# A two-layer hybrid backbone: the order of the whole program from the scheduler's finer duration model

## The chip, the cores and the metric

One core of one Trainium2 chip runs the whole program in one launch. The metric is the device time of one execution in microseconds (us); the median of three runs of the kernel before is 3073.74 us (3067.39 to 3075.61).

## The reference

The reference computes two layers of a backbone for a diffusion generator on 1024 latent tokens and 256 context tokens of width 1024, all in float32. Cut to what matters:

```python
for i in range(2):                                   # layers; context is dropped after the first
    sh1, sc1, g1, sh2, sc2, g2 = split(silu(c) @ w_mod + b_mod)
    h = rms_norm(x, norm1_gain) * (1 + sc1) + sh1    # the same for the context tokens
    aq, ak, av, bq, bk, bv, cx, cg = split(h @ w_in)
    ya = diff_attention(...)    # 4 heads: softmax(q0 k0) - lam * softmax(q1 k1), all 1280 keys
    yb = window_attention(...)  # 6 heads: 256 context keys, 3 blocks of 128 keys, a sink
    yc = rglru(cx) * gelu(cg)   # a linear recurrence in both directions
    x = x + g1 * (concat(ya, yb, yc) @ w_out)
    h2 = rms_norm(x, norm2_gain) * (1 + sc2) + sh2
    gate, val = split(h2 @ w_up)                     # 2 x 2816 columns
    x = x + g2 * ((silu(dwconv(gate)) * val) @ w_down)
```

## The kernel before, in words

Every large matrix product is made in three passes: each factor is split in a rounded high part (`hi`, L184, on ACT) and the rest (`lo`, L187, on DVE or POOL), and high x high, high x low and low x high are added up in one PSUM bank. Each layer runs through these stages:

- **Phase A** (`phase_a`): norm, the input projection (`qkv`, L636 to L638), rope and per-head norms (`qk_post`), and the recurrence (`lru`). In the second layer the end of the first layer's down product (`tail`) comes ahead of it.
- **Phase B** (`phase_b`): windowed attention (`sw`), then differential attention (`da`). `da` is written as a software pipeline over query tiles, and it puts pieces of other work (modulation products, a part of the output projection) between its steps.
- **Phase C** (`phase_c`): output projection, second norm (`norm_ops`), then `up(f)` for 22 blocks of 128 gate and value columns, a Strassen-like scheme of seven products of sums of quarters (`t1` to `t4` are made on POOL, L1524, the activation sums on DVE, L1250 to L1264), and `down_steps`, the same scheme for the down product: five steps of seven products, each product's sums on POOL (L1342), splits on ACT, DVE and POOL, its result added from PSUM by DVE (L1380 into the residual, L1412 into a collected sum `a`). In the first layer the context tokens' products (`dc_ps`, L1425 to L1427) stand between them.

**What sets the order.** The kernel is written in a framework that has one in-order queue for each engine: PE (matmul), DVE, ACT, POOL, and SP, which issues most DMAs. The text of the kernel gives each instruction a place in the program. A scheduler then plays the program through before the launch: whenever a simulated engine is free, it takes the first instruction in program order whose inputs are ready and whose buffer is free at that simulated time. So an instruction can go ahead of one that stands before it in the program, if the simulation thinks that the earlier one has to wait. What comes out is a fixed order for each queue, with waits on semaphores. On the chip an engine never passes over an instruction that waits: what stands behind it waits too.

How long the simulation thinks that an instruction or a transfer takes decides the order. There are two such models. The coarse one is the default. The finer one follows an instruction through sequencer, queue, engine and semaphores. Before the change the finer one is asked for in one place, a block of its own around phase A of each layer and the tail ahead of it:

```python
    def layer(self, l):
        ...
        with self.tc.block(schedule_with_timeline_sim=True):
            if l:
                self.tail()
            self.phase_a()
        self.phase_b()
        self.phase_c()
```

A block is ordered by itself: nothing in it changes places with what stands outside. So the program falls into a short setup, block A of layer 0, phases B and C of layer 0 as one stretch, block A of layer 1 with the tail, and phases B and C of layer 1. Setup and the two B and C stretches were ordered with the coarse model.

The scheduler also gives out buffers in the order of its simulation. The tags that the prediction speaks of have few slots: PSUM has two banks of tag `t` and six of tag `p` in phase C.

## Time and profile before

| what | value |
|---|---|
| runs | 3067.39, 3073.74, 3075.61 us |
| the profiled execution | 3074.54 us, span 3072.8 us |
| mean granted TensorE clock | 0.972 of full speed |
| PE busy | 2836.2 us (92% of the span) |
| DVE, POOL, ACT busy | 2070.9 (67%), 1520.2 (49%), 1468.6 us (48%) |
| DMA | 349.25 MB, mean 114 GB/s |

The stages lie in the span about so: phase A of layer 0 from 0 to 337.5 us, windowed attention to 466, differential attention to 707, output projection and norm to 865, `up` to 1368, `down_steps` to 1661, tail and phase A of layer 1 to 1985, attention, output projection and norm of layer 1 to 2470, `up` to 2812, `down_steps` to 3046, and the last two of the 22 blocks to 3072.8.

A timeline row gives start, duration, engine, line, operation, the tile that is written and what is read; in square brackets stands how long the engine sat idle before it and what ended the wait. PE's busy time counts pipelined matmuls as one stretch. At full clock a 512-column matmul starts 0.23 us after the one before it.

### The profile page before, as it was taken

How to read it: one execution, taken by the hardware profiler on the slowest of the kernel's cores; microseconds unless marked ns; L12 is line 12 of the kernel's file. 1: busy time of each engine (PE TensorE's matmuls, PEld its weight loads, DVE VectorE, ACT ScalarE, POOL GpSimd, SP SyncE). 2: the span in 40 equal slices, each digit the busy share in tenths (PEclk: the TensorE clock that was granted, in tenths of full speed). 3: DMA queues.
4: the chain of work that ended last, by engine and by line, in shares of the span. 5: the costliest groups of instructions: out<-in, count | busy, mean ns of one | idle time of the engine just before them, and what ended most of it. 6: DMA issues, size and time to landing. Idle time of an engine off the chain costs nothing. (4 is left out here: it accounts for less than half of the span.)

```text
span 3072.8 us, 40965 instructions
## 1 busy us (share of the span) xinstructions
PE 2836.2 (92%) x15146; PEld 2308.8 (75%) x15146; DVE 2070.9 (67%) x2879; ACT 1468.6 (48%) x2450; POOL 1520.2 (49%) x1011
## 2 busy tenths in 40 slices
PE   6999898999899999998988899898999799999898
PEld 4798665678688888886877788666777678887776
DVE  6956656884854444457887985757885755556997
ACT  5544467784443433342332554567883444444331
POOL 4746412323554444448561765512323576665971
PEclk9999999999899999998999999999999999999999
DMA  7232627664122111143215331545533122224322
GB/s 254 83 85 82 173 61 248 185 196 172 38 81 76 67 68 67 67 182 113 83 56 192 112 109 52 145 109 168 130 121 131 55 89 83 83 83 158 123 83 83
DMA packets 208280, 349.25 MB, mean 114 GB/s; under 512 B 32720, under 2 KB 112336, under 8 KB 208080
## 3 DMA queue, kind: packets, MB, share of 16 engines
q1 hardware_dynamic: 203472, 331.69, 33.3%
q0 software_dynamic: 4608, 14.95, 2.2%
q8 instruction: 119, 1.95, 0.3%
q14 instruction: 81, 0.66, 0.1%
HBM read 257.19 MB, written 89.39 MB: 113 GB/s over the span
## 5 line engine op out<-in xcount | busy, mean ns | idle before, releaser
L184 ACT ACTIVATE w_r<-w_raw 128x512 fp32r<-128x512 f32 x338 | 212.7, 631 | 451.4 <-PE u_ps L1552 279.7
L1524 POOL TENSOR_TENSOR w_raw<-w_raw 128x512 f32<-128x512 f32 x176 | 249.9, 1425 | 229.3 <-DVE w_r L187 108.5
L187 DVE TENSOR_TENSOR w_r<-w_raw,w_r 128x512 fp32r<-128x512 f32 x206 | 151.3, 737 | 250.2 <-ACT w_r L184 250.1
L1551 PE MATMUL u_ps<-a,w_r 128*128 128x512 f32 x704 | 278.6, 396 | 5.1 <-DVE vb L1639 4.0
L1552 PE MATMUL u_ps<-a,w_r 128*128 128x512 f32 x704 | 277.5, 394 | 1.4 <-DVE a L187 1.2
L1553 PE MATMUL u_ps<-a,w_r 128*128 128x512 f32 x704 | 276.3, 392 | 0.0
L187 POOL TENSOR_TENSOR w_r<-w_raw,w_r 128x512 fp32r<-128x512 f32 x132 | 190.2, 1441 | 122.7 <-ACT w_r L184 117.5
L1403 PE MATMUL d_ps<-d_ah,d_b 128*128 128x512 f32 x560 | 225.2, 403 | 22.5 <-DVE xd L1380 12.3
L1404 PE MATMUL d_ps<-d_al,d_b 128*128 128x512 f32 x560 | 223.9, 400 | 6.2 <-DVE d_al L187 6.2
L946 DVE TENSOR_REDUCE da_sm<-da_s 128x1 f32<-128x1280 f32 (+1 forms) x144 | 194.9, 1367 | 43.6 <-PE da_s L936 42.7
L1405 PE MATMUL d_ps<-d_ah,d_b 128*128 128x512 f32 x560 | 223.3, 399 | 0.6 <-DVE d_b L187 0.6
L187 POOL TENSOR_TENSOR w<-raw,w 128x1024 fp32r<-128x1024 f32 (+2 forms) x62 | 141.1, 2283 | 144.1 <-ACT w L184 135.1
L953 ACT ACTIVATE da_e<-da_s,da_sm 128x1280 f32<-128x1280 f32 (+1 forms) x144 | 177.6, 1235 | 22.9 <-DVE da_sm L946 21.2
L1551 PEld LDWEIGHTS u_ps<-a,w_r 128*128 128x128 f32 x704 | 133.9, 190 | 34.6 <-DVE vb L1639 5.5
L1090 POOL TENSOR_TENSOR oy_x<-oy_x,oy_z 128x426 f32<-128x426 f32 (+3 forms) x48 | 52.1, 1086 | 216.3 <-ACT oy_z L1088 193.7
L1552 PEld LDWEIGHTS u_ps<-a,w_r 128*128 128x128 f32 x704 | 133.9, 190 | 29.5 <-DVE a L187 2.1
L1553 PEld LDWEIGHTS u_ps<-a,w_r 128*128 128x128 f32 x704 | 133.6, 190 | 28.8
L1380 DVE SCALAR_TENSOR_TENSOR xd<-d_ps,mods,xd 128x512 f32<-128x512 f32 x200 | 141.0, 739 | 19.7 <-PE d_ps L1405 19.4
L1403 PEld LDWEIGHTS d_ps<-d_ah,d_b 128*128 128x128 f32 x560 | 108.7, 194 | 48.3 <-DVE xd L1380 10.0
L936 PE MATMUL da_s<-dak,daq 96*128 96x512 f32 (+1 forms) x400 | 123.0, 395 | 13.7 <-ACT da_e L953 13.3
L1639 DVE TENSOR_TENSOR vb<-u_ps,vb 128x512 f32<-128x512 f32 x96 | 66.0, 688 | 99.2 <-PE u_ps L1553 90.5
L1551 PE MATMUL u_ps<-s_x,w_r 128*128 128x512 f32 x308 | 122.0, 396 | 10.1 <-ACT s_x L184 10.1
(349 smaller groups left out, 8616.3 us busy)
## 6 DMA issues: line engine op xcount, KB each, us to landing
wmod<-in_wmod SPq DMA_DIRECT2D x96, 512.0 KB, 6.5
w_raw<-in_wu SPq DMA_DIRECT2D x44, 1024.0 KB, 5.4
d_w<-in_wd SPq DMA_DIRECT2D x40, 512.0 KB, 3.9
d_a<-ud SPq DMA_DIRECT2D x40, 512.0 KB, 4.6
ud<-conv SPq DMA_DIRECT2D x22, 640.0 KB, 2.9
ud<-conv SPq DMA_DIRECT2D x22, 512.0 KB, 2.6
raw<-in_wg SPq DMA_DIRECT2D x16, 512.0 KB, 4.1
dak<-qk_da POOLq DMA_DIRECT2D x48, 160.0 KB, 4.6
```

Of the source, the lines that this page charges most:

```text
L184: self.nc.scalar.activation(out, in_, AF.Copy)
L187: (eng or self.nc.vector).tensor_tensor(out, in_, hi.bitcast(F32), ALU.subtract)
L946: nc.vector.tensor_reduce(st["sm"][:, mi:mi + 1], st["s"][mi][:, :b["nkc"]], AX.X, ALU.max, negate=True)
L953: nc.scalar.activation(e[:, :nkc], st["s"][mi][:, :nkc], AF.Exp, bias=st["sm"][:, mi:mi + 1], accum_out=b["s0"][:, ti, u["hd"], mi:mi + 1])
L1380: nc.vector.scalar_tensor_tensor(x, ps, gate, x, ALU.mult, ALU.add)
L1403: nc.tensor.matmul(ps, bh[:, w], ah[:, m], start=on is None and k == 0, stop=False, **kw)
L1404: nc.tensor.matmul(ps, bh[:, w], al[:, m], start=False, stop=False, **kw)
L1405: nc.tensor.matmul(ps, bl[:, w], ah[:, m], start=False, stop=k == 1, **kw)
L1524: sub = lambda o, a, b, op=ALU.subtract: nc.gpsimd.tensor_tensor(o, a, b, op)
L1551: nc.tensor.matmul(ps, wh[:, s], h, start=new and kk == 0, stop=False, skip_group_check=not new)
L1552: nc.tensor.matmul(ps, wh[:, s], lo, start=False, stop=False, skip_group_check=not new)
L1553: nc.tensor.matmul(ps, wl[:, s], h, start=False, stop=kk == 3, skip_group_check=not new)
```

## The change

One argument is given to the context that holds the whole program. Setup and both stretches of phases B and C are then ordered with the finer model too. No instruction is added or taken away, no tile changes its size; what changes is the order within each engine's queue, the buffers' turns, and with them the waits. The blocks stay, and nothing moves over their edges.

```diff
-    with tile.TileContext(nc) as tc:
+    with tile.TileContext(nc, schedule_with_timeline_sim=True) as tc:
         Build(tc, aps).run()
```

## Rows read from the trace of the kernel before

**Rows 1.** The page's first part: busy us, share of the span, instructions.

```profile
PE 2836.2 (92%) x15146; PEld 2308.8 (75%) x15146; DVE 2070.9 (67%) x2879; ACT 1468.6 (48%) x2450; POOL 1520.2 (49%) x1011
```

**Rows 2.** Windows by stage: length, busy PE, PEld, DVE, ACT, POOL; clock, DMA share, GB/s.

```profile
60.00:337.50 277.50, 262.37 (x1241) 224.21 (x1240) 200.85 (x264) 131.91 (x190) 176.90 (x98) 0.98 0.33 91
337.50:865.00 527.50, 476.27 (x3129) 363.15 (x3128) 360.40 (x618) 333.71 (x677) 161.75 (x158) 0.96 0.48 150
865.00:1368.00 503.00, 503.00 (x2672) 433.41 (x2671) 240.49 (x335) 203.67 (x326) 243.01 (x181) 1.00 0.23 82
1368.00:1661.00 293.00, 263.18 (x1329) 222.30 (x1327) 238.84 (x288) 84.88 (x99) 173.75 (x78) 0.96 0.30 99
1661.00:1985.00 324.00, 295.29 (x1416) 250.47 (x1414) 244.46 (x331) 158.70 (x233) 193.83 (x111) 0.95 0.41 121
1985.00:2470.00 485.00, 430.00 (x2771) 330.62 (x2772) 342.30 (x507) 300.96 (x567) 157.64 (x154) 0.96 0.41 122
2470.00:2812.00 342.00, 342.00 (x1497) 280.85 (x1496) 176.81 (x216) 147.78 (x231) 225.91 (x156) 1.00 0.26 90
2812.00:3046.00 234.00, 207.44 (x852) 166.14 (x851) 215.68 (x201) 76.60 (x79) 168.63 (x59) 0.94 0.31 101
```

**Rows 3.** Timeline of DVE, then PE, at the start of layer 0's down product.

```profile
1392.69 2.28 DVE L187 TENSOR_TENSOR d_al<-d_s,d_ah 128x1024 fp32r<-128x1024 f32 x1 [5.97 <-ACT d_ah L184]
1394.89 0.47 DVE L1380 SCALAR_TENSOR_TENSOR xd<-dc_ps,mods,xd 128x256 f32<-128x256 f32 x1
...
1395.42 0.58 PE L1425 MATMUL dc_ps<-d_ah,d_b 128*128 128x256 f32 x1 [6.72 <-DVE xd L1380]
```

**Rows 4.** Timeline of DVE, then PE, in layer 1's down product.

```profile
2873.51 2.39 DVE L187 TENSOR_TENSOR d_b<-d_t,d_b 128x1024 fp32r<-128x1024 f32 x1 [4.49 <-ACT d_b L184]
2875.83 0.68 DVE L1412 TENSOR_TENSOR a<-d_ps,a 128x512 f32<-128x512 f32 x1
...
2876.56 0.80 PE L1403 MATMUL d_ps<-d_ah,d_b 128*128 128x512 f32 x1 [6.00 <-DVE a L1412]
```

**Rows 5.** Timeline of DVE, then PE, near the end of layer 1.

```profile
3005.45 1.23 DVE L187 TENSOR_TENSOR ul<-ul,uh 128x1024 fp32r<-128x1024 f32 x1 [5.94 <-ACT uh L184]
3006.59 0.74 DVE L1380 SCALAR_TENSOR_TENSOR xd<-d_ps,mods,xd 128x512 f32<-128x512 f32 x1
...
3007.39 0.80 PE L1403 MATMUL d_ps<-d_ah,d_b 128*128 128x512 f32 x1 [5.94 <-DVE xd L1380]
```

**Rows 6.** Windows behind those three waits, and one wait in the norm; columns as before.

```profile
1395.20:1401.00 5.80, 5.58 (x20) 5.00 (x21) 2.31 (x5) 1.43 (x2) 5.80 (x3) 0.51 0.62 190
2876.50:2882.50 6.00, 5.94 (x15) 4.66 (x16) 6.00 (x8) 2.00 (x2) 6.00 (x3) 0.52 0.21 75
3007.40:3014.00 6.60, 6.60 (x20) 5.25 (x21) 6.60 (x7) 1.74 (x2) 2.44 (x1) 0.66 0.24 79
2400.70:2411.10 10.40, 0.27 (x3) 0.02 (x1) 10.40 (x13) 4.93 (x8) 5.06 (x3) 0.68 0.00 1
```

**Rows 7.** PE's groups by line: context products of layer 0's down stage.

```profile
L1425 PE MATMUL dc_ps<-d_ah,d_b 128*128 128x256 f32 x160 | 49.7, 311 | 27.1 <-DVE xd L1380 26.3 <-DVE a L1412 0.8
```

**Rows 8.** Timeline of PE: the longest waits of the two norm stages.

```profile
830.04 0.69 PE L399 MATMUL n_bc<-cst_all,nr 128*128 128x128 f32 x2 [5.30 <-POOL nr L396]
...
2411.08 0.80 PE L1551 MATMUL u_ps<-s_x,w_r 128*128 128x512 f32 x1 [10.13 <-ACT s_x L184]
```

**Rows 9.** Timeline of PE: a wait in phase A of layer 1.

```profile
1968.49 0.88 PE L699 MATMUL qk_t<-cst_all,qa 128*128 128x128 f32 x3 [6.30 <-DVE qa L694]
```

**Rows 10.** Timeline of POOL in layer 1's down product.

```profile
2866.82 3.26 POOL L1342 TENSOR_TENSOR d_s<-d_a,d_s 128x1024 f32<-128x1024 f32 x1
2870.04 2.35 POOL L1342 TENSOR_TENSOR d_t<-d_w 128x1024 f32<-128x1024 f32 x1
```

**Rows 11.** Timeline of DVE, then PE, early in layer 1's up stage.

```profile
2443.78 2.24 DVE L1676 TENSOR_TENSOR conv<-conv,vb 128x1024 f32<-128x1024 f32 x1
...
2446.68 0.50 PE L1551 MATMUL u_ps<-a,w_r 128*128 128x512 f32 x1 [1.98 <-DVE vb L1639]
```

## The prediction, made before the change was run

> **What bounds the kernel now.** I read the page's busy shares first: PE is busy 92% of the span, the next engine, DVE, 67% [rows 1]. So PE sets the time on the whole, and what can be won is time in which PE stands still or runs slowly; its work itself is the same under any order. The second view is the windows by stage, cut where the order changes its model [rows 2]. The reader is to see three kinds of stages there.
>
> The two `up` stages have PE busy for 503.00 of 503.00 and 342.00 of 342.00 us. The change reorders them, and nothing can be won in them.
>
> The other stages that are to be reordered (337.5 to 865, 1368 to 1661, 1985 to 2470, 2812 to 3046) leave PE idle for 51.2 + 29.8 + 55.0 + 26.6 = 162.6 of 1539.5 us, which is 10.6%.
>
> The stages that the finer model orders already (60 to 337.5, past the first loads, and 1661 to 1985) leave it idle for 15.1 + 28.7 = 43.8 of 601.5 us, which is 7.3%. They are other code, so this is a hint and no proof.
>
> The third view is the timeline at the longest idle stretches of PE, to see whether the work itself or its place in a queue made PE wait. Three of them are questions of place alone:
>
> At 1388.7 us PE waits 6.72 us for a bank that DVE empties in 0.47 us (`xd<-dc_ps`). DVE stands idle 5.97 us ahead of that on a split, `d_al<-d_s`, whose input comes late through ACT, and the short add is queued behind it [rows 3]. At 2870.6 it is the same with `d_b<-d_t` in front and the add into `a` (0.68 us) behind it: PE waits 6.00 us [rows 4]. At 3001.5 DVE stands on `ul`, a split of the last stage that waits for a load, while the add that PE needs (0.74 us) is behind it: 5.94 us [rows 5]. In each the coarse model believed the input to be there sooner than the chip has it. That is the sort of error that better durations mend.
>
> **The change part by part.** It adds and removes no instruction and no transfer; it moves them. I make the sum against the profiled execution, 3074.5 us, 0.8 us above the median of the runs shown.
>
> *The three blockages.* Their idle time is 6.72 + 6.00 + 5.94 = 18.7 us. Behind each, PE runs for some 6 us at a granted clock of 0.51, 0.52 and 0.66 of full speed, that is mostly at 1.2 instead of 2.4 GHz [rows 6]; against full clock that is 5.8 x 0.49 + 6.0 x 0.48 + 6.6 x 0.34 = 8.0 us more. Together 26.7 us. If the finer model sees the input late, DVE does the short add first and PE goes on. What is late next is DVE itself: in the last down stage it is busy 215.7 of 234 us [rows 2], and the split that it stood on still has to be made. So I count two thirds, 18 us. The bounds are 0, if the finer model errs alike, and 26.7.
>
> *Context products.* In layer 0's down stage the first matmul of each context product waits 27.1 us in all for DVE [rows 7]; less the 6.72 us above, that is 20.4 us in many small waits. The next product's matmuls are often ready meanwhile and stand behind it in PE's queue. A model that sees DVE's add as late lets them pass. They need free banks, so I take half, 10 us; bounds 0 and 20.4.
>
> *The norm stages.* PE waits 5.30 us for a factor that comes through DVE and POOL, and 10.13 us for a split of `s2` [rows 8]. During the second DVE is busy for 10.40 of 10.40 us [rows 6]: the chain is real work, and only a few products could be put into the gap. I take a third of 15.4 us, 5 us; bounds 0 and 15.4.
>
> *Attention.* The long stretches 337.5 to 865 and 1985 to 2470 hold 106 us of idle time [rows 2]; of that 15.4 us are counted above, and the rest is spread thinly over a pipeline written out by hand. A freer order may close some waits and open as many. I take 0. The nearest rows bound it: at the finer stages' 7.3% these two stretches (906.3 us busy) would idle 71 us, 35 less than now; and the same distance the other way.
>
> *Transfers.* SP's queue is reordered too, each issue with what is behind it in that queue. The DMA engines are busy 0.23 to 0.48 of the time in the reordered stages [rows 2], so an earlier or later issue is mostly hidden. I take 0, inside the bounds above; it shows first where a split waits for a load, as `ul` does.
>
> *`up`.* I take 0. The bounds are 0 and the loss under the first rival below.
>
> The sum is 18 + 10 + 5 = 33 us: 3074.5 - 33 = 3041.5, so **3042 us**.
>
> A page that speaks against a part of this is the Trainium skill's "SBUF — State Buffer", section "Who interferes with whom": a DVE instruction with two SBUF inputs and a GpSimd instruction that reads SBUF share a port, and whichever comes second is held up until the other ends. The trace agrees that the same POOL sum takes 2.35 us in one place and 3.26 us in another [rows 10]. A scheduler that takes each instruction's time alone would be wrong there under either model; that is the third rival.
>
> **The rivals.**
>
> *Slower: the `up` stages lose their unbroken stream.* A bank of `up` is free when DVE has added it into `vb`. At 2444.7 us that add is queued behind a 2.24 us product `conv`, and PE waits 1.98 us [rows 11]. This is an order that occurs at the start of layer 1's `up` and not later. There are 2 x 22 rounds; if the new order puts the add behind the product in each, they cost 44 x 1.98 = 87 us, and with the 33 us won the time is 3074.5 - 33 + 87 = 3129 us. It decides from 17 rounds on (33 / 1.98). For it speaks that PE has no slack there; against it that DVE is busy only 240.5 of 503 and 176.8 of 342 us [rows 2], so that a good order is easy to find. Chance 0.2.
>
> *Slower: as many long waits as the finer stages have.* In the 601.5 us ordered by the finer model there are four waits of PE of over 4 us (5.87, 5.91, 4.35 and 6.30 us; the last is [rows 9]); at that rate the 1539.5 us would have ten, and they have five now [rows 3 to 5, 8]. Five more at some 5.6 us, and 2.7 us each at a low clock as in the three above, are 41 us: 3116 us, if nothing else is won. Against it: the last of these waits is the end of a block, which the reordered stretches have only once per layer. Chance 0.16.
>
> *No change, by POOL's durations.* Two of the three blockages hang on sums made by POOL [rows 3, 4], which take 2.35 us or about 0.9 us more, as DVE's work happens to lie [rows 10]. If the finer model takes the short time, a split is still placed too early in many of the 70 products of the two down stages; one such delay in every second product, 35 x 0.9 = 32 us, eats the whole gain: 3074 us. By that page's rule this is what happens. Long waits that change places (four new ones of 8.3 us) give the same time. Chance 0.15 together. That the argument does not reach the stretches outside the blocks, so that each queue keeps its order and the time is 3074 us, has 0.02: they stand directly in the context that gets it.
>
> **How the numbers follow.** About 0.3%, 9 us, is what a measurement of this kernel can tell from no change. The forecast has 0.47, the two slower rivals 0.36, no change 0.17. The forecast's own range is 3010 to 3063: the upper end is a third of the gain, the lower one the three upper bounds together, 26.7 + 20.4 + 15.4 = 62.5 us. The whole range reaches down to 2992, where all four stages idle as little as the better finer one (15.1 of 277.5 us, 5.4%; 1376.9 us busy then idle 79 us, 83 less than now), and up to 3130 for the first rival.
>
> **What would show it.** Right: PE's idle time in the two down stages falls from 56 us to about 34 (56.4 less two thirds of 18.7 and 10), no short DVE add stands behind a split that waits, `ul` is split behind the last adds, and `up` stays at full busy time in both layers. Wrong: idle time in `up` with `vb` as the releaser (first rival), more waits of PE of over 4 us than five in attention and norm (second), or the same sum of idle time with the waits at other places and POOL's sums as their origin (third). If every queue has its old order, the change did nothing.

## The result, and the profile after

The change makes the kernel slower. The median of four runs is 3120.75 us (3119.1 to 3121.73) against 3071.0 us (3067.39 to 3075.61) in four runs of the kernel before, a ratio of 1.0161, interval [1.0143, 1.0178]. The forecast was 3042 us, faster; the time lies in the range, on the other side of no change.

The page's first part, which answers [rows 1], shows little: PE is busy 38 us longer in a span that is 47 us longer.

```profile
PE 2874.3 (92%) x15146; PEld 2322.2 (74%) x15146; DVE 2101.8 (67%) x2879; ACT 1463.3 (47%) x2450; POOL 1525.7 (49%) x1011
```

So the stages have to be laid side by side. In this table a stage runs from its first instruction on PE to that of the next, in us, layer 0 / layer 1, read from the two profiled executions. "sw" is windowed, "da" differential attention.

| stage | before | after | difference |
|---|---|---|---|
| phase A, with the tail | 341.2 / 314.3 | 339.6 / 311.1 | -1.6 / -3.2 |
| sw | 126.6 / 109.3 | 142.6 / 122.3 | +16.0 / +13.0 |
| da | 242.9 / 205.1 | 267.2 / 213.2 | +24.3 / +8.1 |
| output projection, norm, `up` | 657.9 / 521.4 | 670.0 / 526.0 | +12.1 / +4.6 |
| down, to the end | 298.3 / 252.3 | 276.1 / 248.6 | -22.2 / -3.7 |

The down stages won 26 us; attention lost 61 and the stretch from output projection to `up` 17. The windows of after by stage (length, busy PE, PEld, DVE, ACT, POOL, clock, DMA share, GB/s) answer to [rows 2]:

```profile
339.60:482.20 142.60, 122.82 (x703) 84.14 (x702) 72.13 (x188) 73.85 (x195) 18.22 (x44) 0.94 0.42 101
482.20:749.40 267.20, 231.38 (x1693) 165.57 (x1691) 195.91 (x291) 189.10 (x368) 73.25 (x63) 0.96 0.59 188
836.00:905.00 69.00, 50.20 (x213) 40.10 (x212) 57.71 (x78) 34.62 (x67) 38.90 (x30) 0.80 0.07 26
905.00:1419.00 514.00, 512.68 (x2713) 441.07 (x2712) 256.17 (x345) 208.53 (x335) 250.07 (x186) 1.00 0.22 80
1419.00:1690.00 271.00, 257.64 (x1327) 217.56 (x1325) 245.00 (x288) 84.51 (x98) 183.22 (x78) 0.99 0.32 107
2006.50:2128.80 122.30, 107.61 (x620) 75.53 (x621) 61.92 (x152) 63.19 (x155) 16.79 (x40) 0.95 0.46 113
2128.80:2342.00 213.20, 186.76 (x1471) 145.19 (x1469) 170.35 (x218) 164.01 (x299) 61.43 (x61) 0.98 0.48 138
2409.00:2520.00 111.00, 92.86 (x357) 71.85 (x358) 84.91 (x111) 48.39 (x76) 52.47 (x36) 0.86 0.16 53
2520.00:2864.00 344.00, 344.00 (x1500) 281.37 (x1499) 194.09 (x215) 148.43 (x230) 231.07 (x156) 1.00 0.26 91
2864.00:3090.00 226.00, 204.64 (x828) 160.85 (x827) 217.88 (x199) 76.95 (x79) 170.89 (x59) 0.95 0.32 103
```

In the down stages PE idles 271.0 - 257.6 + 226.0 - 204.6 = 34.7 us, where it was 56.4. In layer 1 DVE is now busy for 217.88 of 226.00 us. `up` keeps its stream: 344.00 of 344.00 us, and 512.68 of 514.00. For attention the same windows of before, which the prediction had not cut out, are:

```profile
341.20:467.80 126.60, 112.11 (x706) 81.57 (x706) 71.68 (x188) 77.11 (x196) 18.24 (x44) 0.96 0.45 112
467.80:710.70 242.90, 223.69 (x1713) 161.81 (x1713) 188.12 (x288) 190.30 (x368) 76.72 (x64) 0.99 0.62 200
1981.20:2090.50 109.30, 95.47 (x627) 70.89 (x628) 62.14 (x152) 67.35 (x162) 18.39 (x41) 0.98 0.50 127
2090.50:2295.60 205.10, 185.42 (x1486) 143.69 (x1485) 168.02 (x215) 163.22 (x294) 61.31 (x62) 0.97 0.48 141
```

PE's idle time in the four grew from 67.2 to 96.7 us, and its busy time for the same instructions from 616.7 to 648.6 us. Part of the latter is the clock: busy time times what is missing from full clock is 14 us before and 26 us after. Most of the rest comes with the number of stops: the profile counts the matmul ahead of a stop as busy up to its modelled end (0.28 us on average in after), where the next one would else have started within that time. Less the usual distance of like matmuls in the traces this is an estimated 19 us before and 34 after. The idle time comes in small pieces. Counting every stop of PE of over 0.1 us in attention, there were 114 before and 194 after; those under 1.5 us went from 104 with 45 us to 187 with 77 us. The long ones did not multiply.

**What changed in the queue.** Attention is a chain: PE makes scores (`sw_s`, `da_s`), DVE their maximum, ACT the exponentials, PE transposes these four at a time into a bank of tag `t` (`sw_t`, `da_t`), ACT empties the bank (`sw_w`, `da_w`), PE multiplies by the values (`sw_pv`, `da_pv`). The scores of `da` have two buffers in PSUM. Tag `t` has two banks, which the products of the output projection (`oy_ps`), the modulation and the value products use too. PE's order in the middle of windowed attention, first before, then after:

```profile
404.64 0.93 PE L846 MATMUL sw_t<-cst_all,sw_p 128*128 128x128 f32 x7
405.32 0.48 PE L866 MATMUL sw_s<-swk,swq 128*128 128x256 f32 x2
405.71 0.66 PE L846 MATMUL sw_t<-cst_all,sw_p 128*128 128x128 f32 x4
406.13 0.37 PE L871 MATMUL sw_s<-mask_r,ident_r 128*128 128x256 f32 x1
406.33 0.40 PE L873 MATMUL sw_s<-swk,swq 128*128 128x256 f32 x2
```

```profile
409.32 0.55 PE L828 MATMUL sw_pb<-cst_all,sw_rb 128*128 128x128 f32 x3
410.45 1.25 PE L846 MATMUL sw_t<-cst_all,sw_p 128*128 128x128 f32 x8 [0.58 <-ACT sw_pbs L830]
411.85 0.66 PE L846 MATMUL sw_t<-cst_all,sw_p 128*128 128x128 f32 x4 [0.15 <-ACT sw_w L857]
412.62 0.50 PE L866 MATMUL sw_s<-swk,swq 128*128 128x256 f32 x2
```

Before, scores stand between the transposes, and PE has work while ACT empties a bank. After, three groups of transposes stand in a row, and with two banks the third has to wait until ACT has emptied the first (0.15 us here). In a step near the end of differential attention in layer 0 it costs more, first before, then after:

```profile
681.25 0.66 PE L291 MATMUL mod_t<-cst_all,mod_m 128*128 128x128 f32 x4
681.66 0.83 PE L936 MATMUL da_s<-dak,daq 96*128 96x512 f32 x3
682.33 1.04 PE L977 MATMUL da_t<-cst_all,da_e 128*128 128x128 f32 x8
683.12 0.47 PE L936 MATMUL da_s<-dak,daq 96*128 96x512 f32 x1
683.62 0.44 PE L977 MATMUL da_t<-cst_all,da_e 128*128 128x128 f32 x2
```

```profile
723.88 1.44 PE L936 MATMUL da_s<-dak,daq 96*128 96x512 f32 x6
725.16 0.60 PE L291 MATMUL mod_t<-cst_all,mod_m 128*128 128x128 f32 x4
725.60 0.60 PE L977 MATMUL da_t<-cst_all,da_e 128*128 128x128 f32 x4
726.89 0.66 PE L977 MATMUL da_t<-cst_all,da_e 128*128 128x128 f32 x4 [0.69 <-ACT da_w L978]
729.24 0.44 PE L977 MATMUL da_t<-cst_all,da_e 128*128 128x128 f32 x2 [1.69 <-DVE mods L293]
```

After has made its scores ahead, in one piece, and has none to put between. Not every step shows it: in the next one before stands idle for 0.35 and 1.21 us, and after for 0.93 and 0.99. Over the whole of `da`, PE's waits ahead of transposes grow from 3.9 to 12.3 us in layer 0 and from 3.3 to 6.6 in layer 1, and its waits ahead of scores from 5.1 to 14.7 and from 8.3 to 10.3. I call the number of score groups that PE's queue holds ahead of a group's transposes the *lead* (in `sw` counted in head groups, in `da` in steps). Read from the order of the queues in the two programs:

| | before | after |
|---|---|---|
| mean lead in sw, layer 0 / 1 | 2.5 / 2.5 | 3.7 / 3.7 |
| mean lead in da | 2.35 / 2.5 | 4.5 / 4.2 |
| rows of three groups of transposes in da | 2 / 2 | 15 / 9 |
| the same in sw | 2 / 2 | 13 / 13 |

A row of three is a stretch of more than eight transposes with nothing between them. So two things changed together, the lead and the rows.

That they cost the time is the theory that the runs below test. Its first rival was that nothing is systematic: that any new order moves attention by tens of us.

### The profile page after: what moved, and what is told of

Read it like the earlier page. It is cut to its first block, busy times and chain, and to the rows that moved or that the text cites. A ratio compares the mean times of both kernels' runs of the same rounds, so it can differ in the third digit from the quotient of the medians.

```text
span 3119.9 us, 40832 instructions
## 1 busy us (share of the span) xinstructions
PE 2874.3 (92%) x15146; PEld 2322.2 (74%) x15146; DVE 2101.8 (67%) x2879; ACT 1463.3 (47%) x2450; POOL 1525.7 (49%) x1011
## 5 line engine op out<-in xcount | busy, mean ns | idle before, releaser
L1524 POOL TENSOR_TENSOR w_raw<-w_raw 128x512 f32<-128x512 f32 x176 | 240.3, 1366 | 247.5 <-DMA w_raw<-in_wu 122.5
L187 DVE TENSOR_TENSOR w_r<-w_raw,w_r 128x512 fp32r<-128x512 f32 x206 | 179.4, 873 | 181.8 <-ACT w_r L184 181.7
L187 POOL TENSOR_TENSOR w_r<-w_raw,w_r 128x512 fp32r<-128x512 f32 x132 | 197.9, 1500 | 112.1 <-ACT w_r L184 105.5
L1403 PE MATMUL d_ps<-d_ah,d_b 128*128 128x512 f32 x560 | 222.0, 403 | 18.0 <-DVE xd L1380 9.1
L1405 PE MATMUL d_ps<-d_ah,d_b 128*128 128x512 f32 x560 | 218.2, 399 | 1.9 <-POOL d_b L187 1.7
L936 PE MATMUL da_s<-dak,daq 96*128 96x512 f32 (+1 forms) x400 | 111.3, 387 | 25.7 <-ACT da_e L953 25.0
L1404 PEld LDWEIGHTS d_ps<-d_al,d_b 128*128 128x128 f32 x560 | 108.7, 194 | 32.8 <-DVE d_al L187 11.6
```

Source lines behind the costliest of these rows:

```text
L187: (eng or self.nc.vector).tensor_tensor(out, in_, hi.bitcast(F32), ALU.subtract)
L1403: nc.tensor.matmul(ps, bh[:, w], ah[:, m], start=on is None and k == 0, stop=False, **kw)
L1404: nc.tensor.matmul(ps, bh[:, w], al[:, m], start=False, stop=False, **kw)
L1405: nc.tensor.matmul(ps, bl[:, w], ah[:, m], start=False, stop=k == 1, **kw)
L1524: sub = lambda o, a, b, op=ALU.subtract: nc.gpsimd.tensor_tensor(o, a, b, op)
```

## The experiments

Stages of all runs, from their profiles, layer 0 / layer 1 in us; "rest" is output projection, norm and `up`; "ratio" is to the kernel before, measured beside each run. A profiled execution can be some us from its median (e1's took 3043.2 us, e2's 3145.8). The code cuts leave out guards for the first and last steps.

| kernel | sw | da | rest | down | median, ratio |
|---|---|---|---|---|---|
| e1 after's down | 126.5 / 109.7 | 242.6 / 206.4 | 658.1 / 521.2 | 275.0 / 245.4 | 3050.35, 0.9916 [0.9901, 0.9931] |
| e2 after's early part | 143.1 / 121.8 | 269.7 / 212.8 | 667.8 / 524.2 | 293.4 / 251.3 | 3152.1, 1.0252 [1.0234, 1.0271] |
| e3 blocks, coarse | 126.2 / 108.9 | 253.4 / 219.8 | 653.1 / 522.3 | 297.3 / 250.2 | 3094.45, 1.0066 [1.0051, 1.0081] |
| e4 blocks, fine A and B | 142.6 / 122.8 | 285.1 / 227.1 | 648.4 / 516.8 | 296.3 / 251.2 | 3149.79, 1.0248 [1.0228, 1.0269] |
| e5 fine, short lead | 128.6 / 110.8 | 276.1 / 233.9 | 665.7 / 524.3 | 278.8 / 247.8 | 3129.29, 1.0183 [1.0159, 1.0206] |
| e6 fine, middle lead | 129.9 / 112.9 | 277.2 / 239.4 | 665.0 / 525.1 | 277.8 / 248.4 | 3138.12, 1.0211 [1.0194, 1.0228] |
| e7 coarse, long lead | 132.1 / 116.6 | 274.8 / 219.4 | 656.2 / 517.5 | 297.9 / 251.9 | 3133.76, 1.0193 [1.0177, 1.0208] |
| e8 fine, interleaved | 128.2 / 111.2 | 257.5 / 193.8 | 664.4 / 521.9 | 278.9 / 248.2 | 3064.14, 0.9956 [0.9941, 0.9971] |
| e9 coarse, rows | 126.6 / 110.3 | 257.8 / 214.9 | 655.9 / 522.4 | 299.2 / 250.8 | 3092.97, 1.0053 [1.0036, 1.0070] |
| e10 coarse, interleaved | 127.7 / 109.5 | 253.0 / 214.0 | 656.1 / 521.9 | 298.9 / 253.1 | 3095.3, 1.0066 [1.0049, 1.0083] |
| e11 best of each | 126.6 / 112.0 | 242.6 / 193.3 | 658.1 / 521.7 | 276.1 / 245.8 | 3039.53, 0.9889 [0.9874, 0.9904] |

**e1 and e2: where the time goes.** Each instruction of phases B and C is tied to the one ahead of it in a recorded order. `NOSYNC` stands here and below for a tie that orders the issue and adds no wait. The context keeps the coarse model.

```diff
         self.phase_c()
+        self.pin()
+    def pin(self):
+        at = {i.name: i for i in self.nc.cur_bb.bb.instructions}
+        for seq in ORDER[self.l].values():          # one list for each engine
+            for a, b in zip(seq, seq[1:]):
+                self.tc.add_manual_dep(at[f"I-{b}"], f"I-{a}", NOSYNC, reason="pin")
```

> Every queue of phases B and C is pinned to a recorded order: up to block 7 of `up` the order of the kernel before, from block 8 of `up` to the end of the down stage the order of the kernel after. Theory (each stage's time comes from its own order; the finer order wins in the down stages and loses in attention and norm): down stages 276 and 222 us long instead of 298 and 230, attention as before (sw 127 and 109, da 243 and 205), whole 3071 - 30 = 3041 us. Rival (the stages' gains hang on the state in which the stage ahead leaves buffers and transfers): down stages near 298 and 230, whole near 3071 us.

> The mirror image: attention, output projection, norm and `up` to block 7 in the order of the kernel after, the rest in the order of the kernel before. Theory: sw 143 and 122, da 267 and 213, norm and `up` some 15 us longer in all, down as before: 3121 + 30 = 3151 us, so that both mixtures together are as far from the kernel before as the kernel after is (+47 us). Rival (the loss comes from phase A's new order, which this kernel doesn't have): attention near 127, 243, 109, 205 and the whole near 3071 us.

Both came out as the theory had it: 3050 us (expected 3041) and 3152 (expected 3151), and each stage has the length that its order has in the kernel it comes from, within 4 us but for layer 0's down stage in e2 (293.4, before 298.3). In e2 phase A of layer 0 has the order of before, and attention behind it is as long as after's: the loss is made in attention itself. The down windows of e1, to be read against [rows 2], where PE idled 29.8 and 26.6 us (here 12.5 and 20.4):

```profile
1368.00:1635.00 267.00, 254.49 (x1312) 215.51 (x1312) 244.49 (x285) 84.49 (x98) 184.69 (x77) 0.99 0.32 105
2790.00:3011.00 221.00, 200.56 (x821) 159.11 (x822) 211.07 (x198) 76.03 (x78) 173.96 (x59) 0.95 0.31 101
```

**e3 and e4: a second sample of each model.** An outer block around A and B, plain in e3, with the finer model in e4; C is left to the coarse one.

```diff
-        with self.tc.block(schedule_with_timeline_sim=True):
-            ...
-        self.phase_b()
+        with self.tc.block():      # e4: block(schedule_with_timeline_sim=True)
+            with self.tc.block(schedule_with_timeline_sim=True):
+                ...
+            self.phase_b()
         self.phase_c()
```

> Phases A and B of a layer stand together in a plain block with the coarse model (A in its own finer block inside it, as before); phase C stays outside. No model changes, but every queue gets another order, since the edge between B and C can't be crossed. It is a second sample of what the coarse model makes of attention. Theory (the coarse model orders attention well): sw and da together within 10 us of the 684 us of before; whole 3071 to 3090 with the new edge. Rival (chance: any reordering moves attention by tens of us): sw and da together 700 us or more.

> As the kernel with plain blocks, but the block around A and B asks for the finer model, so that attention alone is ordered finely and C coarsely. A second sample of what the finer model makes of attention. Theory (the finer model orders attention badly): sw and da together within 15 us of the 745 us of after, whole 3071 + 61 = 3132 us, with the edge 3130 to 3150. Rival (chance): sw and da together under 710 us.

`sw` has 126.2 / 108.9 and 142.6 / 122.8 us, to 0.5 us the values of before and after. But this is hardly a second sample. Read from the traces by tiles, PE's order in `sw` is the very order of before in layer 1 of e3 and that of after in layer 0 of e4, and nearly so in the other two: each model made its own order again. So the pair shows that the loss comes back with the model, and not what another order would cost.

In `da` e3 is 10.5 and 14.7 us longer than before, so that attention takes 708.3 us, by the letter the rival's case, and e4's 777.6 us is above my 745 +- 15. That is the edge and not the order: the last steps of attention, 72 matmuls in each layer, can no longer move behind it into the output projection and count in the stage. From the first scores to the end of the last value products `da` takes 252.6 / 213.8 us before, 247.5 / 213.9 in e3, 279.2 / 221.3 in e4 and 283.6 / 229.2 after. With the same edge the finer model is 31.7 and 7.3 us longer in `da`, as it is 24.3 and 8.1 without it.

**e5 and e6: the kernel after with a bound on the lead.**

```diff
+            behind = self.heads[-4]            # sw: last transpose of head group h - 4 (e6: h - 3)
+            with self.tc.issue_after(behind):
                 ...                            # the score matmuls of group h
+            behind = state[n - 3]["last"]      # da: last transpose of step n - 3 (e6: n - 4)
+            with self.tc.issue_after(behind):
                 ...                            # the score matmuls of step n
```

> The kernel after, with a bound on how far PE's queue puts scores ahead of the transposes that use them: in windowed attention the scores of head group h stand behind the transposes of group h - 4 (mean lead 2.8 groups; before 2.5, after 3.7), in differential attention the scores of step n behind the transposes of step n - 3 (mean lead 2.4 steps; before 2.35 and 2.5, after 4.5 and 4.2). Theory (the long lead of the finer order is what costs): sw within 5 us of 127 and 109, da within 8 us of 243 and 205, so whole 3121 - 61 = 3060, 3050 to 3075 us. Rival (the loss comes from other parts of the order: the late load of the queries, the queues of ACT and DVE): sw and da together still over 725 us of after's 745, whole over 3100 us.

> As the kernel with the short lead, with other bounds: windowed attention behind group h - 3 (mean lead 1.95 groups), differential attention behind step n - 4 (mean lead 3.35 and 3.2 steps). Theory: da lies between, near 255 and 209 us; sw is no longer than with the bound of 4, unless a lead of two groups is too short for the exponentials, then longer. Rival: da 267 and 213 as in the kernel after.

`sw` falls to 128.6 / 110.8 us, 2 us from before: the bound takes back 14.0 of 16.0 us and 11.5 of 13.0. Rows of three fell with the lead there, from 13 / 13 to 0 / 1, so these runs do not part the two. The late load of the queries, which the rival names, is not the loss: in layer 0 PE waits 5.5 us for it in after and still 4.4 in e5. In `da` the theory failed as I had put it, and by sum and total the rival holds: with before's lead the stage got *longer*, 276.1 and 233.9 us, and e6, with a lead between, is no better. The waits of PE in layer 1's `da` say why (us in total, times, longest); e5:

```profile
PE da_t L984 <- ACT oy_z L1096: 17.9, 22, 1.9
PE da_t L984 <- DVE da_o L760: 9.3, 14, 1.0
PE da_t L984 <- ACT da_w L986: 5.6, 11, 1.1
```

All three release banks of tag `t`. My bound held all scores behind the *last* transposes of a step, so that all ten stand unbroken: rows of three rose from 15 / 9 to 30 / 29. It had mended the lead and taken away the scores between the transposes.

**e7: the kernel before with after's lead.** For each group and step, its transposes are tied behind the scores that stood ahead of them in the kernel after.

```diff
+        for n, d in enumerate(LEAD[self.l]):       # d: the lead of step n in the kernel after
+            self.tc.add_manual_dep(state[n]["first"], state[n + d]["score", 0].name, NOSYNC, reason="lead")
```

The head groups of `sw` are tied in the same way.

> The kernel before (coarse model), with after's lead forced on it: each group of transposes stands in PE's queue behind the scores that stood ahead of it in the kernel after, group by group in windowed attention and step by step in differential attention (mean leads 3.7 groups, 4.3 and 4.1 steps). Everything else is left to the coarse model. Theory (the lead is the cause): sw near 143 and 122, da near 267 and 213, the later stages as before, whole 3073 + 61 = 3134 us. Rival (the lead is only a mark of the finer order, something else costs): sw and da stay within 15 us of the 684 us of before, whole under 3090 us.

The lead, forced on the coarse order, costs 31.9 and 14.3 us in `da`, more than the finer model's order does, and 3134 us in all. It is not quite alone: rows of three came with it, 16 / 21 where before has 2 / 2. The total is as expected by luck in part, since `da` is 7.8 and 6.4 us longer than forecast and `sw` 10.9 and 5.4 us shorter. In `sw` lead and rows as in after (rows 14 / 13) cost 5.5 and 7.3 of the 16.0 and 13.0 us: there they are a part of the cause, and in the finer order more hangs on them. PE's largest waits in layer 0's `da`, before, after and e7, in that order, point to the lead and not to the rows:

```profile
PE da_s L936 <- ACT da_e L953: 5.1, 7, 2.1
```

```profile
PE da_s L936 <- ACT da_e L953: 14.7, 21, 1.4
```

```profile
PE da_s L950 <- ACT da_e L968: 23.3, 18, 3.2
```

Scores that are to be made early wait for their own bank, which ACT's exponentials of an earlier step still read, and the transposes behind them wait with them. All waits ahead of transposes are 5.2 us in that stage of e7.

**e8 and e9: the order between the transposes.** e8 is the kernel after with the bound of e5 in `sw` and a fixed order in `da`; e9 is the kernel before with rows of three at a short lead. `behind(i, j)` ties `i` behind `j`.

```diff
+        for n in range(ns):                                # e8
+            t, k = state[n]["t"], n + 2
+            behind(state[k]["s", 1][0], t[3])              # second map of step n + 2 behind four transposes
+            behind(t[4], state[k]["s", 1][-1])             # the others behind that map
+            behind(state[k + 1]["s", 0][0], t[-1])         # first map of step n + 3 behind all
+        for n in range(ns):                                # e9
+            behind(t[0], state[k]["s", 1][-1])
+            behind(state[k + 1]["s", 0][0], t[-1])
```

> The kernel after, with the short lead in windowed attention (scores of group h behind the transposes of group h - 4) and, in differential attention, a fixed pattern on PE: the first four transposes of step n, then the second score map of step n + 2, then the other transposes of step n, then the first score map of step n + 3. So no three groups of transposes stand in a row (before 2 such rows of three in layer 0, after 15, the kernel with the short lead 30). Theory (PE waits because a row of transposes needs more than the two banks that ACT empties; scores between them are the work that fills this): da within 8 us of 243 and 205, sw 129 and 111 as with the short lead, whole 3121 - 14 - 12 - 24 - 8 = 3063 us, 3055 to 3080. Rival (the finer order of ACT and DVE, not of PE, costs): da stays at 265 and 212 or more, whole 3090 us or more.

> The kernel before (coarse model) with the short lead of two to three steps kept in differential attention, but with the pattern broken: both score maps of step n + 2 stand ahead of all transposes of step n, and those of step n + 3 behind them, so that the ten transposes of a step stand in three groups in a row (30 such rows in each layer). The rest is left to the coarse model. Theory (the rows cost, at any lead): da 270 to 280 and 225 to 237, as in the finer kernel with 30 rows, the other stages as before, whole near 3073 + 33 + 25 = 3131 us. Rival (rows cost only together with the finer order): da within 10 us of 243 and 205, whole under 3085 us.

e8 gives 3064 us, 57 less than after and less than before, by ties on PE alone; the scheduler set the other queues anew around them. `da` in sum is 451.3 us (before 448.0, after 480.4), but not layer by layer: 257.5 is 15 us above before and 193.8 is 11 below. Against e5, with the same model and the rows, it is 18.6 and 40.1 us. PE's waits ahead of transposes are 16.6 and 10.9 us, in e5 25.8 and 35.0. The first two in layer 1's `da`, to be read against e5's above:

```profile
PE da_t L983 <- ACT oy_z L1108: 4.9, 12, 0.8
PE da_t L983 <- DVE da_o L760: 3.2, 5, 1.2
```

All in all these waits are longer than in after (12.3 and 6.6). What e8 has less of is the other wait: scores wait 1.6 us in layer 0 and never over 0.15 us in layer 1, where after has 14.7 and 10.3 us in all. So what it wins over after points to the lead.

e9 is 14.9 and 9.8 us above before: in layer 0 half of what theory gave, in layer 1 within the rival's 10 us. What part of that the rows have, e10 shows.

**e10 and e11.** e10 puts e8's order in `da` on the coarse kernel. e11 pins, as in e1, layer 0 as before and layer 1 as e8 up to block 7 of `up`, then after's order in both.

> The kernel before (coarse model) with the fixed pattern of the finer interleaved kernel in differential attention; nothing else is bound. It completes the table of two models and two patterns. Theory (the pattern on PE, not the model of the other queues, sets da): da as in the finer kernel with it, 257 and 194 us within 6, all other stages as before, so whole 3073 + 14 - 11 = 3076, 3068 to 3085 us. Rival (the order of ACT and DVE counts as much): da at least 10 us away from these in one layer.

> Every queue of phases B and C pinned: layer 0 in the order of the kernel before up to block 7 of `up`, layer 1 up to there in the order of the finer interleaved kernel, and from block 8 to the end of the down stage in the order of the kernel after in both layers. Theory (each stage's time is that of its own order): the 3050 us of the kernel with after's down stages, less 9 us that layer 1's attention, output projection, norm and `up` took less in the finer interleaved kernel: 3041 us, 3033 to 3050, faster than all kernels so far. Rival (the gains don't add): 3050 us or more.

e10 speaks against the theory in its strong form. The table of `da` by model and pattern, with a short lead of some two steps in all four:

| | scores between | rows of three |
|---|---|---|
| coarse | 253.0 / 214.0 (e10) | 257.8 / 214.9 (e9) |
| finer | 257.5 / 193.8 (e8) | 276.1 / 233.9 (e5) |

With the coarse model rows cost only 4.8 and 0.9 us; with the finer one 18.6 and 40.1. The rest of e9's loss is there without rows too: e10 is 10.1 and 8.9 us above before. So a new order moves a stage of `da` by some 10 to 15 us either way, and after's loss is larger than that in layer 0 (24.3) and not in layer 1 (8.1). With scores between, the two models are 20 us apart in layer 1, which passes the rival's 10 us. PE waits in e10's layer 1 for other things than in e8:

```profile
PE da_s L936 <- ACT da_e L954: 7.8, 8, 1.3
PE da_pv L752 <- ACT da_w L980: 6.8, 13, 1.2
```

ACT's queue differs: in e8 the first exponentials of step n + 2 stand ahead of the emptying of step n's banks in all 38 and 30 steps, in e10 in 12 and 7. That ACT's queue carries the 20 us is not shown, for DVE's and POOL's queues differ too.

e11 came out at 3039.5 us (expected 3041), 1.1% faster than before and the fastest of all. The stages add up once more.

## Why the prediction was wrong

- **The step that failed is "Attention. ... I take 0"**, with its bounds of 35 us either way. It was +61 us. The idle time there was spread over 114 short stops, and I took this as neutral, since a freer order "may close some waits and open as many". But the text of the kernel is a pipeline by hand, and the coarse order kept to it: lead of two to three, scores between transposes. The finer model lets scores run ahead by 4.5 and 4.2 steps, where PE waits for their banks (14.7 us in layer 0, before 5.1). Forcing that lead on the coarse order costs more still (e7), and taking it back with scores between the transposes wins 29 of the 32 us of `da` in sum (e8). What lead, rows and ACT's queue each have of the loss stays open in `sw`, and layer by layer in `da`. My bounds came from the idle share of phase A, other code, and counted idle time alone: that grew by 29.5 us, inside the 35, and the other half of the loss (31.9 of 61 us) is busy time.
- **The blockages and the context products were right, and so was their sum.** The three waits of [rows 3 to 5] are gone, the idle time of the down stages is 34.7 us where I wrote "about 34", and the context products' first matmuls, 27.1 us in [rows 7], wait 5.2:

```profile
L1425 PE MATMUL dc_ps<-d_ah,d_b 128*128 128x256 f32 x160 | 46.8, 292 | 5.2 <-DVE xd L1380 5.1
```

  The split `ul` now stands between the last adds, as forecast, and DVE goes from one to the next without idling:

```profile
3051.19 0.74 DVE L1380 SCALAR_TENSOR_TENSOR xd<-d_ps,mods,xd 128x512 f32<-128x512 f32 x1
3051.85 2.73 DVE L187 TENSOR_TENSOR ul<-ul,uh 128x1024 fp32r<-128x1024 f32 x1
3054.50 1.40 DVE L1380 SCALAR_TENSOR_TENSOR xd<-d_ps,mods,xd 128x512 f32<-128x512 f32 x2
```

  The sum was 18 + 10 = 28 us; after has 25.9 and e1, where nothing else changes, 23.0 in its median. By layer it was not right, so the sum is luck in part: two thirds of each blockage and the context products are 16 us in layer 0 and 11 in layer 1, and after has 22.2 and 3.7 (e1 23.3 and 6.9). In layer 1 what was "late next" is DVE, as I wrote, but by more: PE's longest wait there is now 4.31 us at 2910.8, for a split `d_al` that comes late though DVE works without a pause ahead of it.
- **The norm had the wrong sign.** I took 5 us of gain; the stretch from output projection to `up` is 12.1 and 4.6 us longer. PE's idle time in it grows from 17.3 to 24.5 us in layer 0: the 5.30 us wait of [rows 8] is 5.85 now, and two of 3.0 and 2.2 us have come up behind it. In layer 1 the 10.13 us wait is gone, but waits of 3.9, 2.2 and 3.6 us stand in its stretch instead, and idle time falls only from 24.8 to 23.0. In the norm's two windows above PE's clock is 0.80 and 0.86, where before had 0.86 and 0.94 in the same stage (794.3 to 865 and 2364.4 to 2470), and in e4, where phase C is coarse, nothing is lost there. Why the finer order is worse in it was not tested.
- **The rivals.** The time is near that of the two slower ones (3129 and 3116 us), but by neither way. `up` did not lose its stream. Waits of over 4 us did not multiply: in the whole span, past the first, they fell from ten to five. The loss came from many short ones, which no rival counted. The third, that POOL's times eat the gain of the down stages, did not happen in sum, since their idle time fell from 56.4 to 34.7 us; how far POOL has a hand in layer 1's small gain was not tested.

## What to carry to other kernels

A stage that idles in many short stops can be a pipeline in balance, not slack: a change that reorders it needs its own price, with both signs, and the worst case is not the idle share of other code. Compare two orders stage by stage from the first instruction of each, and then by how far a producer runs ahead, what stands between instructions that share few buffers, and how the queue of the engine that empties them is ordered (e8 against e10). Where a new scheduler wins one stage and loses another, give each stage the order that suits it: here that made 3071 us into 3040, while the switch for the whole program made 3121.

## What the runs showed of the hardware

Short stops too can go with a lower granted clock, not only long ones as in [rows 6]. In layer 1's `da` PE makes the same matmuls in 177.99 us of busy time at a mean of 0.99 of 2.4 GHz (e8), idling 15.8 us in all, and in 193.54 us at 0.94 (e5, the kernel with rows of three), idling 40.4 us; the means are made of stretches at 2.4 and at 1.2 GHz:

```profile
2095.60:2289.40 193.80, 177.99 (x1486) 139.44 (x1486) 167.64 (x215) 164.14 (x294) 60.43 (x62) 0.99 0.51 148
```

```profile
2112.00:2345.90 233.90, 193.54 (x1462) 145.68 (x1460) 178.43 (x218) 162.83 (x291) 63.25 (x61) 0.94 0.41 120
```

So 15.6 of the 40.1 us between them are no idle time at all; the clock's share, taken as busy time times what is missing, is 193.54 x 0.06 - 177.99 x 0.01 = 9.8 us.

It is no rule by the sum of idle time: in layer 0's `da` e5 idles 47.2 us at a mean of 0.96, and e8 30.9 us at 0.95.
